# The forgetting attention's projections and attention given out ahead of the selecting attention's

## The chip, the cores and the metric

The kernel runs on one NeuronCore of a Trainium2 chip. The metric is the device time of one execution in microseconds. The kernel before took 1939.16 us, the median of three runs (1939.14 to 1940.99).

## The reference

The reference runs two layers of a first block and then a second block over one sequence of 256 tokens, 1024 wide, in fp32. The change lies in the first block. There a normed row x is multiplied with one wide matrix `w_in` (1024 x 3404), whose columns are cut into the inputs of four attentions of 4 heads x 64:

- A, the selecting attention: q, k, v (columns 0 to 767) and an indexer with 8 heads (768 to 1351). `score = sum_h iw_h * relu(iq_h . ik)`; of each row only the 64 best of its earlier keys take part in the softmax.
- B, the forgetting attention: q, k, v (1352 to 2119) and four columns b (2120 to 2123); the log of a sigmoid of b is summed along the sequence, and the difference of the sums at query and key is added to the logits.
- C, the differential attention (2124 to 2891): two softmaxes on 32 dimensions, the first minus lambda times the second, times v, then an rmsnorm per head.
- D, a sliding window of 128 keys with a sink (2892 to 3403).

The four outputs, side by side 1024 wide (`mix`: A, B, C, D), go through `w_out`, a norm and the residual; then come a 4096-wide MLP with squared relu, and a gated per-layer input.

## The kernel before, in words

The tokens are two row tiles (t = 0, 1) of 128. A weight is loaded in pieces of 1024 columns a partition (`wraw`, SP's queue, 4 buffers) and split in two fp32r parts: `whi` by ACT (L102) and the rest `wlo` by DVE (L103), 6 buffers each. The activations are held transposed and split in the same way (`phl`). A projection `proj(c0, n)` (L268) makes three matmuls per 128 rows of the weight (hi x hi, lo x hi, hi x lo): 24 for a row tile, 48 in all, into one of four accumulating PSUM banks per row tile. Another four banks serve everything else.

The side work, the attentions, are Python generators, put into a list by `push`. Each `mm_tok` advances the first two of the list by one step after 12 matmuls (`tick`), so attention steps are strewn in between the matmuls of the projection that follows; `until` steps them to their end. The list that results is put in order per engine by a scheduler, and each engine executes its instructions in that order: an instruction that waits holds all that stand behind it on its engine.

In `layer1` the order before is: the indexer's projections (768 and 1280), whose rope (L485 to L488) and transposes give `iqT` and `ikT` (L363); `index(t)` is pushed, which makes the index scores (matmul L517, relu L520, weighted sums L523), then takes the best 64 in eight rounds of MAX8 and MATCH_REPLACE8 on DVE (L529, L530), and turns the rest into a mask (L533, L534). Then come A's q, k (`proj(0, 512)`) and v, and A's attention is pushed; then the b columns and C's q (`proj(2120, 260)`), B's k, v (`proj(1608, 512)`), and B's attention is pushed; then C and D. An attention's step makes scores (L386), adds the mask and takes the maximum (L387, DVE), exponentials (L398, ACT), transposes of the probabilities (L411, copied by L413) and the product with v (L419). When A and B are done, `transpose_in` (L249; the split copies are L230 and L231) turns their part of `mix` for `w_out`; C's output goes through its norm (L574) first.

Of the kernel before, what the change touches and what calls it, by code (L numbers as in the profile page):

```python
# [17 lines left out]
P = 128  # L18
# [111 lines left out]
class Net:  # L130
# [448 lines left out]
    def layer1(self, i, xT):  # L579
# [20 lines left out]
        def proj(c0, n, get=None):  # L600
            get = get or self.w.cols(w_in, c0, n)
            res = []
            for t in range(NT):
                ps = self.bank(self.acc)[:, :n]
                n0 = 6 if self.early else KT
                self.mm_tok(ps, xT, t, range(n0), get, stop=n0 == KT)
                self.flush()
                if n0 < KT:
                    self.mm_tok(ps, xT, t, range(n0, KT), get, start=False)
                self.early = False  # L610
                res.append(ps)
            return res

        def keep(tag, ps, n, t):
            o = wk.tile([P, 256], F32, name=tag, tag=tag)[:, :n]
            nc.scalar.activation(o, ps, AF.Copy, scale=rstd[t])
            return o

        def roped(tag, pss, n, d):
            res = []  # L620
            for t in range(NT):
                o = wk.tile([P, 512 if n == 512 else 256], F32, name=tag, tag=tag)[:, :n]
                self.rope(o, pss[t], d, t)
                res.append(o)
            return res

        def q_alone(q, rows=64):

            qT = [wk.tile([P, 2, 2, P], F32, name="qT", tag="qT") for _ in range(64 // rows)]
            self.tr_alone(lambda r: qT[r // 2][:, r % 2], q, 2, rows)  # L630
            return qT

        def qT_kT(q, k):
            kT = wk.tile([P, 2, S], F32, name="kT", tag="kT")
            qT = []
            for t in range(NT):
                if q:
                    qT += q_alone(q[t])
                self.tr_heads(kT, k[t], t, 2)
            return qT, kT  # L640

        mix = [wk.tile([P, D], F32, name="mix", tag="mix") for _ in range(NT)]
        each = lambda f: [f(t) for t in range(NT)]


        ps = proj(768, 512, self.first if i == 0 else None)
# [4 lines left out]
        ps = proj(1280, 328, self.second if i == 0 else None)  # L651
# [11 lines left out]
        sel = [None] * NT  # L663
# [2 lines left out]
        if i == 0:  # L666
            self.setup1b()
        self.pin(nc.scalar.preload_act_table_set("natural_log_exp_and_others"))
        ps = proj(0, 512)
        q = roped("rq", [p[:, :256] for p in ps], 256, 64)  # L670
        k = roped("rk", [p[:, 256:] for p in ps], 256, 64)
        qTa, kTa = qT_kT(q, k)
        ps = proj(512, 256)
        va = each(lambda t: keep("v", ps[t], 256, t))

        def att_a(t):
            yield from self.attend(t, qTa, kTa, va, lambda h: h, lambda h: sel[t][:, :(t + 1) * P], mix[t][:, 0:256])

        gen_a = self.chain(*each(att_a))
        self.push(gen_a)  # L680


        ps = proj(2120, 260)
        nlf = []
# [13 lines left out]
        ps = proj(1608, 512)  # L698
# [4 lines left out]
        def att_b():  # L703
            pc = self.bank()
            nc.tensor.matmul(pc[:, 0:4], self.upper[:, :P], nlf[0], start=True, stop=True)
            nc.tensor.matmul(pc[:, 4:8], self.upper[:, P:], nlf[0], start=True, stop=False)
            nc.tensor.matmul(pc[:, 4:8], self.upper[:, :P], nlf[1], start=False, stop=True)
            ncum = self.small.tile([P, 2, 4], F32, name="ncum", tag="ncum")
            nc.vector.tensor_copy(ncum, pc[:, :8].rearrange("p (t h) -> p t h", t=2))
            dec = [wk.tile([P, 4, (t + 1) * P], F32, name="dec", tag=f"df{t}") for t in range(NT)]  # L710
            for h in range(4):
                if h % 2 == 0:
                    pr = self.bank()
                o = pr[:, (h % 2) * S:(h % 2 + 1) * S]
                nc.tensor.matmul(o, nlf[0][:, h:h + 1].to_broadcast([P, P]), self.upper, start=True, stop=False,
                                 skip_group_check=True)
                nc.tensor.matmul(o[:, P:], nlf[1][:, h:h + 1].to_broadcast([P, P]), self.upper[:, :P], start=False,
                                 stop=True, skip_group_check=True)
                for t in range(NT):
                    nk = (t + 1) * P  # L720
                    nc.vector.scalar_tensor_tensor(dec[t][:, h, :], o[:, :nk], ncum[:, t, h:h + 1],
                                                   self.causal[:, S - nk:], op0=ALU.subtract, op1=ALU.add)
                if h == 1:
                    yield
            yield
            for t in range(NT):
                yield from self.attend(t, qTb, kTb, vb, lambda h: h, lambda h: dec[t][:, h, :], mix[t][:, 256:512])
                yield
                if t == 0:
                    self.transpose_in(mix[t][:, :512], mT, t, 4)  # L730

        mT = self.new_parts(KT)
        gen_b = att_b()
        self.push(gen_b)


        ps = proj(2380, 512)
# [8 lines left out]
        ps = proj(2892, 512)  # L746
# [172 lines left out]
        for t in range(NT):  # L919
            ps = [self.bank() for _ in range(2)]  # L920
# [581 lines left out]
```

## Time and profile before

| | |
|---|---|
| median of 3 runs | 1939.16 us (1939.14 to 1940.99) |
| profiled execution, its own time | 1937.16 us |
| span in the trace | 1935.4 us |
| mean granted TensorE clock | 0.988 |
| PE busy / weight loads | 97% / 83% of the span |
| DVE / ACT / POOL busy | 68% / 54% / 4% |
| stretch of the attentions in layer 0 / 1 | about 31 to 176 us / 418 to 555 us of the span |

PE is TensorE's matmuls, PEld its weight loads, DVE VectorE, ACT ScalarE. Matmuls overlap: the duration of a row of PE includes its fill, so what a matmul costs in a row of them is the distance between starts. A row's bracket gives the idle time of the engine in front of it and what ended that.

### The profile page before, as it was taken

To read this page: it belongs to the slowest core of one execution; us is meant where nothing else is said; L and a number is where in the kernel's file an instruction comes from. 1 tells how busy PE (TensorE), PEld (TensorE's weight loads), DVE (VectorE), ACT (ScalarE), POOL (GpSimd) and SP (SyncE) were. 2 spreads that over 40 slices of the span, in tenths; PEclk is the share of its full clock that TensorE was granted. 3 is DMA by queue.
4 is the path that set the end of the run, shared out by engine and by line. 5 is a ranking of instruction groups with operands and counts; after the bars stand their busy time and mean duration, and the time that the engine had idled before them with its cause. 6 is when DMAs were issued, how large, how long until landed. Compare 5 with 4: busy or idle time off the path is not lost.

```text
span 1935.4 us, 27780 instructions
## 1 busy us (share of the span) xinstructions
PE 1877.3 (97%) x10282; PEld 1614.0 (83%) x10282; DVE 1306.8 (68%) x2456; ACT 1035.9 (54%) x1743; POOL 77.8 (4%) x127
## 2 busy tenths in 40 slices
PE   7898999999989999999999999999999999999997
PEld 6787878887878888888888988887988888988886
DVE  6866756687776666558666667566558666677555
ACT  5555544564654545566555655554565555655552
POOL 2000000000000000100000000000000000000000
PEclk9998999999999999999999999999999999999999
DMA  7433676554335555655555656664454555656662
GB/s 214 131 112 97 209 241 210 164 179 133 110 123 186 180 203 158 188 162 162 176 179 181 221 174 211 195 186 141 155 170 155 182 182 172 206 168 217 186 193 89
DMA packets 187132, 334.00 MB, mean 173 GB/s; under 512 B 11622, under 2 KB 109078, under 8 KB 186612
## 3 DMA queue, kind: packets, MB, share of 16 engines
q1 hardware_dynamic: 180160, 308.94, 50.4%
q0 software_dynamic: 6528, 23.18, 3.9%
q8 instruction: 81, 1.33, 0.3%
q14 instruction: 55, 0.45, 0.1%
q10 hardware_dynamic: 308, 0.10, 0.0%
HBM read 331.10 MB, written 4.62 MB: 173 GB/s over the span
## 4 chain that ended last, share of the span: by engine, by line
PE 83%; DVE 7%; DMA 4%; ACT 4%; issue 2%; POOL 0%; DVEq 0%; SPq 0%; ACTq 0%; POOLq 0%
PE bank L325 23%; PE bank L284 20%; PE bank L268 13%; PE bank L327 12%; DMA wraw<-in_w_in_dram 3%; DVE wlo L103 2%; PE bank L386 2%; PE bank L419 2%; PE bank L315 2%; PE bank L314 2%; PE bank L313 2%; ACT whi L102 1%; PE bank L249 1%; ACT pr L398 1%; PE bank L411 1%
## 5 line engine op out<-in xcount | busy, mean ns | idle before, releaser
L103 DVE TENSOR_TENSOR wlo<-wraw,whi 128x1024 fp32r<-128x1024 f32 (+1 forms) x628 | 711.0, 1147 | 328.7 <-ACT whi L102 238.6
L102 ACT ACTIVATE whi<-wraw 128x1024 fp32r<-128x1024 f32 (+1 forms) x628 | 608.9, 997 | 346.1 <-PE bank L284 110.2
L325 PE MATMUL bank<-phl,whi 128*128 128x512 f32 x2080 | 532.3, 395 | 0.4 <-ACT whi L102 0.4
L325 PEld LDWEIGHTS bank<-phl,whi 128*128 128x128 f32 x2080 | 374.9, 189 | 69.1 <-ACT whi L102 1.2
L284 PE MATMUL bank<-whi,phl 128*128 128x512 f32 x1280 | 358.2, 395 | 1.7 <-ACT phl L230 1.0
L268 PE MATMUL bank<-whi,phl 128*128 128x512 f32 (+4 forms) x1152 | 341.2, 378 | 4.3 <-ACT whi L102 2.2
L327 PEld LDWEIGHTS bank<-phl,wlo 128*128 128x128 f32 x2080 | 284.2, 190 | 23.2 <-DVE wlo L103 2.7
L327 PE MATMUL bank<-phl,wlo 128*128 128x256 f32 x2080 | 291.8, 283 | 0.6 <-DVE wlo L103 0.6
L284 PEld LDWEIGHTS bank<-whi,phl 128*128 128x128 f32 x1280 | 237.4, 189 | 53.3 <-ACT phl L230 2.9
L268 PEld LDWEIGHTS bank<-whi,phl 128*128 128x128 f32 x1152 | 210.9, 191 | 34.9 <-ACT phl L230 3.8
L268 PE MATMUL bank<-wlo,phl 128*128 128x512 f32 (+4 forms) x576 | 215.4, 376 | 2.4 <-DVE wlo L103 2.3
L284 PE MATMUL bank<-wlo,phl 128*128 128x512 f32 x640 | 206.2, 394 | 0.1
L284 PEld LDWEIGHTS bank<-wlo,phl 128*128 128x128 f32 x640 | 120.2, 188 | 28.8 <-DVE wlo L103 2.8
L268 PEld LDWEIGHTS bank<-wlo,phl 128*128 128x128 f32 x576 | 110.0, 191 | 18.2 <-DVE wlo L103 4.3
L315 PE MATMUL bank<-phl,wlo 128*128 128x256 f32 x304 | 86.3, 284 | 0.0
L314 PE MATMUL bank<-phl,whi 128*128 128x256 f32 x304 | 86.1, 283 | 0.0
L225 POOL TENSOR_TENSOR ry<-ry,mhalf 128x1 f32<-128x1 f32 (+1 forms) x40 | 32.9, 824 | 1309.1 <-DVE ry L224 1301.6
L313 PE MATMUL bank<-phl,whi 128*128 128x256 f32 x304 | 85.5, 281 | 0.0
L313 PEld LDWEIGHTS bank<-phl,whi 128*128 128x128 f32 x304 | 57.7, 190 | 0.2
L314 PEld LDWEIGHTS bank<-phl,whi 128*128 128x128 f32 x304 | 57.3, 189 | 0.2
L315 PEld LDWEIGHTS bank<-phl,wlo 128*128 128x128 f32 x304 | 57.5, 189 | 0.0
L230 ACT ACTIVATE phl<-bank 128x512 fp32r<-128x512 f32 (+2 forms) x60 | 32.8, 571 | 44.0 <-PE bank L249 43.6
(301 smaller groups left out, 1720.9 us busy)
## 6 DMA issues: line engine op xcount, KB each, us to landing
wraw<-in_w_in_dram SPq DMA_DIRECT2D x172, 512.0 KB, 4.6
wraw<-in_w_mlp_up_dram SPq DMA_DIRECT2D x64, 512.0 KB, 4.6
wraw<-in_w_mlp_down_dram SPq DMA_DIRECT2D x64, 512.0 KB, 4.5
wraw<-in_w_ffn_gate_dram SPq DMA_DIRECT2D x44, 512.0 KB, 4.7
wraw<-in_w_ffn_up_dram SPq DMA_DIRECT2D x44, 512.0 KB, 4.5
wraw<-in_w_ffn_down_dram SPq DMA_DIRECT2D x44, 512.0 KB, 4.4
wraw<-in_w_in_dram SPq DMA_DIRECT2D x54, 384.0 KB, 3.8
wraw<-in_w_out_dram SPq DMA_DIRECT2D x32, 512.0 KB, 4.3
```

The costliest lines, as they stand in the source:

```text
L102: first = nc.scalar.activation(hi[:, :n], src, AF.Copy)
L103: ins = nc.vector.tensor_tensor(lo[:, :n], src, hi[:, :n].bitcast(F32), op=ALU.subtract)
L225: nc.gpsimd.tensor_tensor(y, y, self.mhalf[:, :n], op=ALU.pow)
L268: self.order(nc.tensor.matmul(ps, self.part(parts, kt)[x][:, sl], get(kt + kbase)[w], start=start and n == 0, stop=stop and n == len(terms ...
L284: ins = nc.tensor.matmul(pss[j], self.part(parts, kt)[x][:, sl], get(kt + kbase)[w][:, j * 512:(j + 1) * 512], start=start and n == 0, sto ...
L313: self.order(nc.tensor.matmul(ps, wh, xh, start=first, stop=False, **kw), n == 0)
L314: nc.tensor.matmul(ps, wh, xl, start=False, stop=False, **kw)
L315: nc.tensor.matmul(ps, wl, xh, start=False, stop=last, **kw)
L325: self.order(nc.tensor.matmul(flat, get(kt)[0][:, c:c + P], both, start=n == 0, stop=False), n == 0)
L327: nc.tensor.matmul(ps[:, 0], get(kt)[1][:, c:c + P], self.part(parts, kt)[0], start=False, stop=n == len(kts) - 1)
L386: nc.tensor.matmul(o, qs(h), ks(h), start=True, stop=True)
L419: nc.tensor.matmul(po[:, h * 64:(h + 1) * 64], pts[kb][:, h, :], v(kb, h), start=kb == 0, stop=kb == t)
```

## The change

The lines that make A's projections and push its attention move behind those of B. The transposes of `mix[0]`'s first half, which B's attention made for A's and B's columns together, are cut in two: B's generator turns columns 256 to 511, A's turns 0 to 255.

```diff
--- before.py
+++ after.py
@@ -666,19 +666,6 @@
         if i == 0:
             self.setup1b()
         self.pin(nc.scalar.preload_act_table_set("natural_log_exp_and_others"))
-        ps = proj(0, 512)
-        q = roped("rq", [p[:, :256] for p in ps], 256, 64)
-        k = roped("rk", [p[:, 256:] for p in ps], 256, 64)
-        qTa, kTa = qT_kT(q, k)
-        ps = proj(512, 256)
-        va = each(lambda t: keep("v", ps[t], 256, t))
-
-        def att_a(t):
-            yield from self.attend(t, qTa, kTa, va, lambda h: h, lambda h: sel[t][:, :(t + 1) * P], mix[t][:, 0:256])
-
-        gen_a = self.chain(*each(att_a))
-        self.push(gen_a)
-
 
         ps = proj(2120, 260)
         nlf = []
@@ -727,11 +714,28 @@
                 yield from self.attend(t, qTb, kTb, vb, lambda h: h, lambda h: dec[t][:, h, :], mix[t][:, 256:512])
                 yield
                 if t == 0:
-                    self.transpose_in(mix[t][:, :512], mT, t, 4)
+                    self.transpose_in(mix[t][:, 256:512], mT, t, 2, 2)
 
         mT = self.new_parts(KT)
         gen_b = att_b()
         self.push(gen_b)
+
+
+        ps = proj(0, 512)
+        q = roped("rq", [p[:, :256] for p in ps], 256, 64)
+        k = roped("rk", [p[:, 256:] for p in ps], 256, 64)
+        qTa, kTa = qT_kT(q, k)
+        ps = proj(512, 256)
+        va = each(lambda t: keep("v", ps[t], 256, t))
+
+        def att_a(t):
+            yield from self.attend(t, qTa, kTa, va, lambda h: h, lambda h: sel[t][:, :(t + 1) * P], mix[t][:, 0:256])
+            if t == 0:
+                yield
+                self.transpose_in(mix[t][:, :256], mT, t, 2)
+
+        gen_a = self.chain(*each(att_a))
+        self.push(gen_a)
 
 
         ps = proj(2380, 512)
```

PE in layer 0, where the selection's mask is first met, before: bank_758 and bank_806 are the two row tiles of `proj(2120, 260)` (wlo_749 and wlo_755 are its last splits), kT_613, pr_790 and v_730 to A's attention, bank_919 and bank_970 to `proj(1608, 512)`.

```order
L268 MATMUL bank_919<-whi_897,phl_114 128x512
L268 MATMUL bank_970<-whi_897,phl_114 128x512
L268 MATMUL bank_758<-wlo_749,phl_115 128x260
L268 MATMUL bank_758<-whi_754,phl_115 128x260 x2
L268 MATMUL bank_806<-wlo_749,phl_115 128x260
L268 MATMUL bank_806<-whi_754,phl_115 128x260 x2
L268 MATMUL bank_758<-wlo_755,phl_115 128x260
L268 MATMUL bank_806<-wlo_755,phl_115 128x260
L386 MATMUL bank_791<-kT_613,qT_614 128x128
L386 MATMUL bank_796<-kT_613,qT_614 128x128
L411 MATMUL bank_819<-ident_79,pr_790 128x128 x4
L419 MATMUL bank_838<-v_730,pt_824 128x64 x4
```

After, where PE first needs a split that DVE makes behind the rounds: bank_737 to bank_747 are transposes for B's q and k, nlf and bank_866 B's sums and first scores, bank_782 and bank_828 the two row tiles of `proj(0, 512)` with its first split wlo_761.

```order
L268 MATMUL bank_782<-whi_760,phl_114 128x512
L268 MATMUL bank_828<-whi_760,phl_114 128x512
L362 MATMUL bank_752<-ident_79,bk_729 128x128 x2
L692 MATMUL bank_811<-nlf_591,c_upper_288 128x4
L693 MATMUL bank_811<-nlf_591,c_upper_288 128x4
L694 MATMUL bank_811<-nlf_600,c_upper_288 128x4
L702 MATMUL bank_819<-c_upper_288,nlf_591 128x256
L704 MATMUL bank_819<-c_upper_288,nlf_600 128x128
L702 MATMUL bank_841<-c_upper_288,nlf_591 128x256
L704 MATMUL bank_841<-c_upper_288,nlf_600 128x128
L386 MATMUL bank_866<-kT_735,qT_736 128x128
L268 MATMUL bank_782<-wlo_761,phl_114 128x512
```

Before, A's scores, transposes and product stand directly in PE's way at the mask; now what stands there are B's sums and first score, and then A's own projection.

DVE in layer 0, the end of the eight rounds (score_494 and score_502 are the two row tiles), before, with the splits of `proj(2120, 260)` between them and A's first scores behind.

```order
L530 MATCH_REPLACE score_494<-top_659,score_494 128x128
L529 MAX top_664<-score_502 128x8
L103 TENSOR_TENSOR wlo_749<-wraw_746,whi_748 128x260
L530 MATCH_REPLACE score_502<-top_664,score_502 128x256
L103 TENSOR_TENSOR wlo_755<-wraw_752,whi_754 128x260
L533 TENSOR_SCALAR score_494<-score_494 128x128
L533 TENSOR_SCALAR score_502<-score_502 128x256
L534 TENSOR_TENSOR score_494<-score_494,c_causal_287 128x128
L534 TENSOR_TENSOR score_502<-score_502,c_causal_287 128x256
L387 ISA pr_790,mx_789<-bank_791,score_494 128x128
```

After, the same place, with the splits of `proj(0, 512)` (wlo_761 to wlo_779) behind the rounds.

```order
L530 MATCH_REPLACE score_502<-top_661,score_502 128x256
L529 MAX top_656<-score_494 128x8
L529 MAX top_661<-score_502 128x8
L530 MATCH_REPLACE score_494<-top_656,score_494 128x128
L530 MATCH_REPLACE score_502<-top_661,score_502 128x256
L103 TENSOR_TENSOR wlo_761<-wraw_758,whi_760 128x1024
L103 TENSOR_TENSOR wlo_767<-wraw_764,whi_766 128x1024
L103 TENSOR_TENSOR wlo_773<-wraw_770,whi_772 128x1024
L103 TENSOR_TENSOR wlo_779<-wraw_776,whi_778 128x1024
L533 TENSOR_SCALAR score_494<-score_494 128x128
L533 TENSOR_SCALAR score_502<-score_502 128x256
L534 TENSOR_TENSOR score_494<-score_494,c_causal_287 128x128
```

Two 260-wide splits that stood at the last round are now ahead of the rounds, and four 1024-wide ones stand between the last round and the masks.

PE at the end of layer 0's attentions (second row tile), before: bank_1727 is D's product, bank_1745 C's.

```order
L419 MATMUL bank_1727<-v_1399,pt_1705 128x64
L419 MATMUL bank_1727<-v_1397,pt_1698 128x64
L419 MATMUL bank_1727<-v_1399,pt_1705 128x64
L419 MATMUL bank_1745<-v_1164,pt_1718 128x64
L419 MATMUL bank_1745<-v_1166,pt_1725 128x64
L419 MATMUL bank_1745<-v_1164,pt_1718 128x64
L419 MATMUL bank_1745<-v_1166,pt_1725 128x64
L419 MATMUL bank_1745<-v_1164,pt_1718 128x64
L419 MATMUL bank_1745<-v_1166,pt_1725 128x64
L419 MATMUL bank_1745<-v_1164,pt_1718 128x64
L419 MATMUL bank_1745<-v_1166,pt_1725 128x64
L249 MATMUL bank_1781<-ident_79,mix_166 128x128 x4
```

After: pr_1663 are D's probabilities, bank_1730 is C's product, bank_1750 D's.

```order
L411 MATMUL bank_1710<-ident_79,pr_1663 128x128
L411 MATMUL bank_1717<-ident_79,pr_1663 128x128
L419 MATMUL bank_1730<-v_1203,pt_1708 128x64
L419 MATMUL bank_1750<-v_1429,pt_1715 128x64
L419 MATMUL bank_1750<-v_1431,pt_1722 128x64
L419 MATMUL bank_1750<-v_1429,pt_1715 128x64
L419 MATMUL bank_1750<-v_1431,pt_1722 128x64
L419 MATMUL bank_1750<-v_1429,pt_1715 128x64
L419 MATMUL bank_1750<-v_1431,pt_1722 128x64
L419 MATMUL bank_1750<-v_1429,pt_1715 128x64
L419 MATMUL bank_1750<-v_1431,pt_1722 128x64
L249 MATMUL bank_1784<-ident_79,mix_166 128x128 x4
```

C's product, which stood last ahead of the transposes of mix, now stands among D's transposes and ahead of D's product.

## Rows read from the trace of the kernel before

**Rows 1.** PE, DVE, ACT in stretches of layer 0: busy us (count), PEld between; PEclk; DMA

```profile
50.00:70.00 20.00, 17.82 (x131) 16.51 (x129) 19.79 (x81) 7.77 (x16) 0.00 (x0) 1.00 0.23 63
70.00:80.00 10.00, 7.10 (x24) 5.51 (x25) 7.21 (x33) 5.57 (x16) 0.00 (x0) 0.74 0.44 151
80.00:100.00 20.00, 20.00 (x105) 16.68 (x105) 12.00 (x19) 11.89 (x25) 0.00 (x0) 0.96 0.71 228
...
160.00:175.00 15.00, 9.07 (x53) 8.20 (x54) 6.77 (x23) 6.17 (x21) 1.55 (x2) 0.73 0.00 1
```

**Rows 2.** timeline of PE, layer 0 selection: start, us, instruction, [idle before]

```profile
65.73 0.85 PE L268 MATMUL bank<-whi,phl 128*128 128x260 f32 x4
68.39 0.39 PE L268 MATMUL bank<-wlo,phl 128*128 128x260 f32 x1 [1.81 <-DVE wlo L103]
...
72.25 1.48 PE L411 MATMUL bank<-ident,pr 128*128 128x128 f32 x4 [1.32 <-ACT pr L398]
...
81.49 1.12 PE L268 MATMUL bank<-whi,phl 128*128 128x512 f32 x4
```

**Rows 3.** timeline of PE, distances that give prices

```profile
82.68 0.62 PE L268 MATMUL bank<-whi,phl 128*128 128x512 f32 x2
...
83.37 0.62 PE L268 MATMUL bank<-whi,phl 128*128 128x512 f32 x2
...
61.23 0.64 PE L268 MATMUL bank<-whi,phl 128*128 128x260 f32 x4
61.70 0.28 PE L268 MATMUL bank<-wlo,phl 128*128 128x260 f32 x1
...
48.69 1.47 PE L517 MATMUL bank<-ikT,iqT 128*128 128x128 f32 x8
...
49.80 0.82 PE L268 MATMUL bank<-whi,phl 128*128 128x512 f32 x2
```

**Rows 4.** timeline of PE, layer 1 selection

```profile
448.70 0.62 PE L268 MATMUL bank<-whi,phl 128*128 128x512 f32 x2
...
461.06 1.26 PE L268 MATMUL bank<-whi,phl 128*128 128x512 f32 x4
```

**Rows 5.** timeline of PE, end of the attentions, layer 0, then layer 1

```profile
164.00 2.26 PE L419 MATMUL bank<-v,pt 128*128 128x64 f32 x16 [0.48 <-ACT pt L413]
...
166.78 3.73 PE L419 MATMUL bank<-v,pt 128*128 128x64 f32 x16 [0.52 <-ACT pt L413]
...
173.93 1.12 PE L249 MATMUL bank<-ident,mix 128*128 128x128 f32 x4 [3.42 <-DVE mix L574]
...
552.94 1.11 PE L249 MATMUL bank<-ident,mix 128*128 128x128 f32 x4 [3.42 <-DVE mix L574]
```

**Rows 6.** timeline of PE, first matmuls of A's projection, both layers

```profile
31.17 0.47 PE L268 MATMUL bank<-whi,phl 128*128 128x512 f32 x1
...
417.89 0.39 PE L268 MATMUL bank<-whi,phl 128*128 128x512 f32 x1
```

**Rows 7.** DVE's timeline, rope and selection; last, grouped lines: splits, mean ns

```profile
57.13 0.28 DVE L486 TENSOR_TENSOR rope<-bank,cr 128x128 f32<-128x128 f32 x1
...
58.19 0.28 DVE L486 TENSOR_TENSOR rope<-bank,cr 128x128 f32<-128x128 f32 x1
...
58.59 0.28 DVE L529 MAX8 top<-score 128x8 f32<-128x128 f32 x1
...
59.38 0.61 DVE L529 MAX8 top<-score 128x8 f32<-128x256 f32 x2
...
60.55 0.61 DVE L529 MAX8 top<-score 128x8 f32<-128x256 f32 x2
...
440.16 0.28 DVE L529 MAX8 top<-score 128x8 f32<-128x128 f32 x1
...
L103 DVE TENSOR_TENSOR wlo<-wraw,whi 128x1024 fp32r<-128x1024 f32 x516 | 622.6, 1220 | 287.3 <-ACT whi L102 210.4 <-PE bank L327 70.0 <-issue 1.3
```

**Rows 8.** timeline of PE, layer 0, first index scores

```profile
39.41 1.23 PE L517 MATMUL bank<-ikT,iqT 128*128 128x128 f32 x6 [3.27 <-ACT ikT L363]
```

## Prediction

> **What bounds the kernel now.** I read first the page's busy shares, then windows over the attention stretch of both layers, PE's waits, the timelines of PE and DVE at the places these named, and last the grouped lines for prices. PE is busy 97% of the span (the table above), so only the places where it is not can give time back without removing work. The windows find two such places in layer 0 [rows 1], and layer 1 has their like. At 50 to 80 us of the span DVE is busy 19.79 of 20 us while PE has gaps, and then PE's granted clock is 0.74 of 2.4 GHz, that is partly the 1.2 GHz level; at 80 to 100 it is full again. At 160 to 175 PE is busy 9.07 of 15 us, with nothing coming by DMA.
>
> The first place is the selection: eight rounds of MAX8 and MATCH_REPLACE8 for both row tiles, then the attention that needs them. In PE's timeline of layer 0 [rows 2] the last cheap work starts at 65.73; then PE waits on a split that DVE holds behind the rounds (1.81), then on the masked scores and what follows from them (1.32 on their exponentials), and the full-width projection work is back at 81.49. Those 15.76 us hold 12 matmuls 260 wide, 12 x 0.118 = 1.4; four passes of scores, four transposes and eight of the value product at 128 or less, 16 x 0.11 = 1.8; eight 256-wide score passes at twice that, 1.8; three 512-wide matmuls, 0.7. That is 5.7, so 10.1 us are lost. (0.23 for a 512-wide matmul, 0.118 for a 260-wide one: three and four of them between starts [rows 3]; 0.11 for 128 wide is my rounding of the 260-wide one down.) Layer 1 [rows 4]: 448.70 to 461.06 is 12.36 us, with 4.7 of work by the same count; 7.7 lost.
>
> The second place is the end of the attention [rows 5]: the sliding-window product (164.00), the differential product (166.78), and then the transposes of mix wait 3.42 us on DVE, on the norm of the differential output; layer 1 shows the same 3.42 [rows 5].
>
> **The change part by part.** In PE's order A's two projections (0 and 512) and its attention stand behind B's two (2120 and 1608). No matmul is added, and none removed.
>
> *Selection.* What PE can do between the last indexer projection and the first matmul that needs something behind the rounds is now: 48 matmuls 260 wide, 48 x 0.118 = 5.7; four index groups at 1.11 [rows 3] 4.4; 48 matmuls 512 wide, 11.0; eight transposes, the cumulative sums and the first score, about 12 short passes at no more than 0.118, 1.4; two 512-wide ones, 0.5. Together 23.0 us. That work starts where the first matmul of A's projection starts now: at 31.17 and 417.89 [rows 6].
> - When the rounds start: of DVE's work ahead of them, four splits for A's q and k, two for A's v (all 1024 wide) and two 780 wide are replaced by two 780, two 260 and four 1024 wide; A's four rope groups (1.06 each, from one L486 to that of the next group) become two, and eight instructions of four columns come in (about 0.13 each, an estimate: under half of the 0.28 of the 128-wide one). Splits: 6 x 1.22 + 2 x 0.96 = 9.2 before, 4 x 1.22 + 2 x 0.96 + 2 x 0.40 = 7.6 after (the shorter ones scaled by width) [rows 7]; rope 4.2 before, 2.1 after; 1.0 in. DVE has 2.7 less to do, and before it was at MAX8 at 58.59 with hardly a gap: 55.9 in layer 0. In layer 1 DVE waits for the index groups, and these come 48 x (0.23 - 0.118) = 5.4 earlier: between 440.16 - 5.4 = 434.8 and 440.16 - 2.7 = 437.5 [rows 7].
> - When they end: a round takes 1.17 (59.38 to 60.55), eight 9.4; the first of A's splits stands right behind, 1.2 more [rows 7]. So 66.5 in layer 0, 445.4 to 448.1 in layer 1.
> - When PE gets there: layer 0, 31.17 + 23.0 + 2.0 for the transposes of the indexer's q and k, + 3.3 for the wait on ikT that stands in front of the first index group [rows 8] and some 2.2 of half clock behind it (an estimate: six passes there take 1.23, twice their price, and I let that last some 4.4 us) = 61.7. Layer 1, 417.89 + 23.0 + 1.1 = 442.0.
> - What is left to wait: 4.8 in layer 0, 3.4 to 6.1 in layer 1 (I take 4.8), and 1 us each of half clock behind it; 5.8 lost, against 10.1 and 7.7. Gain 4.3 and 1.9. A's scores, which PE now meets only after two 512-wide passes and A's v, no longer wait on the masks: that is inside the two differences. Bounds: 0 when the wait only moves, 10.1 and 7.7 when all of it is covered.
>
> On the page "Perfetto Trace Analysis" of the Trainium skill, section "Identifying the Most-Contended Engine", the engine of highest occupancy is to be improved first, and TensorE is to be judged by its weight loads. By the window 50 to 70, DVE (19.79) stands over PE's weight loads (16.51), so the rule speaks for no gain there, 0 in place of 6.2 us; the same page's "Optimization Strategy" allows that interleaving stretches with different bounds helps, and the trace shows such stretches side by side: DVE full at 50 to 70, PE full at 80 to 100 [rows 1].
>
> *Waits that the order adds.* The four splits of A's projection (4 x 1.22) stand in DVE's queue between the rounds and the masks, and behind them B's decay and scores. PE uses a split in 6 x 0.23 = 1.4 us, more than the 1.22 that DVE needs for one, so once the first is there they don't hold PE; B's first decay rows come some 7 us after the rounds, under 24 matmuls 512 wide (5.5) and A's second pass. I take 0; 2 us a layer at worst.
>
> *DMA.* The weight loads follow the new order on SP's queue: 260-wide columns first, which is less data ahead of the wait on ikT. I take no change, with bounds of -3.3 (the wait gone) and +3.3 (doubled).
>
> *The split transposes.* Two groups of 256 columns in place of one of 512: one instruction more on ACT and on DVE a layer, each under the 1.22 of a 1024-wide split, beside w_out and projection work: 0, at worst 1.2 a layer.
>
> *End of the attention.* In the new PE order the differential transposes come before the last w_out matmuls, the differential product is interleaved with the sliding-window transposes, and the sliding-window product is last. Behind the differential product then stand 2.26 us of work plus its 0.48 of wait [rows 5], under which the norm can run: the 3.42 falls to about 1.0, the sliding-window attention's own short chain (a reciprocal and a product on DVE). Gain 2.4 a layer, 4.8 in all. Bounds: all of 3.42 and the 0.52, 3.9 a layer; or -1, if the earlier differential transposes wait for DVE, which is then behind on the differential's subtraction.
>
> **Sum.** 4.3 + 1.9 + 4.8 = 11.0. The profiled execution took 1937.16, its span of 1935.4 and 1.8 around it; 1937.2 - 11.0 = 1926.2. It stands 2.0 under the median of the runs, 1939.16, so the forecast on that footing is 1928.2, rounded 1928.
>
> **The rivals.**
> 1. *DVE sets the stretch, and the wait moves.* No DVE instruction goes; if its whole chain from the first index scores to the last mask is what ends each time, PE's loss is the same later. For: 19.79 of 20. Against: after the rounds DVE is busy 7.21 of 10 [rows 1], so it has room right behind. Selection 0 and the end 0 to 3: 1936 to 1939, within 0.2%.
> 2. *Slower: the rounds catch PE with nothing in hand.* PE comes to A's first split just as MAX8 starts, because the wait at ikT or for B's second split has already delayed the index groups and with them the rounds. Then PE waits 9.4 + 1.2 and about 3 more at half clock, 13.6 a layer, in place of 10.1 and 7.7: +9.4, less about 2.4 at the end; 1946. It decides when PE is less than about 2 us behind MAX8. For: in layer 0 B's second split stands among the last index sums on DVE, some 6 us before the rounds (three splits, two rope groups). Against: 23 us of work in hand against the 9.4.
> 3. *All is covered.* The rounds end before PE arrives in both layers, and the end keeps its 3.4 a layer: 17.8 + 6.8 = 24.6; 1915. Against: it needs MAX8 5 us earlier than DVE's count gives.
>
> **How the numbers follow.** Two runs of this kernel can be told apart at about 0.2%, 3.9 us. Forecast 0.60, rival 1 0.16, rival 2 0.10, rival 3 0.14. Faster by over 0.2% is the forecast and rival 3, 0.74; same 0.16; slower 0.10. The range goes from rival 3's 1915 to 1941, past rival 1 and the unknown waits; rival 2 is left out, with a little of the low end. The forecast's own range is 1920 to 1934.
>
> **What would show it.** Right: PE's wait on wlo (L103) in front of the first 512-wide matmuls of A, 3 to 6 us a layer; none to speak of on A's masked scores; the granted clock of the stretch above 0.9; the wait of L249 on mix near 1 us, on L494 rather than L574. Wrong: a wait over 9 us on wlo; a wait on mix still at 3.4; new waits on differential transposes (L411 on df) or on B's decay (L386); the index groups or the wait on ikT coming later than now.

## The result, and the profile after

The changed kernel takes 1914.68 us (median of 4 runs, 1913.21 to 1915.68), the kernel before 1939.15 in the same comparison: a ratio of 0.9883, 95% interval 0.9867 to 0.9898. It is 24.5 us faster, where 11.0 were forecast, with 1915 as the low end of the range. A second comparison, further down, gave 1917.07 for it, 21.4 less than the kernel before: sizes of a few us are to be read with that in mind. The profiled execution's span went from 1935.4 to 1911.4.

Where the 24.0 us of the span come from is read at three marks that both kernels have: TensorE's first matmul after the indexer's projections, the first matmul of `w_out` (L284), and the first transposes of `xg` (L249), just behind those of mix. The rows of PE's timeline, before (the first mark is in [rows 6]):

```profile
130.36 0.71 PE L284 MATMUL bank<-whi,phl 128*128 128x512 f32 x2
...
174.84 1.49 PE L249 MATMUL bank<-ident,xg 128*128 128x128 f32 x6
...
510.73 0.70 PE L284 MATMUL bank<-whi,phl 128*128 128x512 f32 x2
...
553.85 1.49 PE L249 MATMUL bank<-ident,xg 128*128 128x128 f32 x6
```

and after:

```profile
30.95 0.29 PE L268 MATMUL bank<-whi,phl 128*128 128x260 f32 x1
...
122.88 0.82 PE L284 MATMUL bank<-whi,phl 128*128 128x512 f32 x2
...
162.31 1.48 PE L249 MATMUL bank<-ident,xg 128*128 128x128 f32 x6
...
405.54 0.28 PE L268 MATMUL bank<-whi,phl 128*128 128x260 f32 x1
...
491.40 0.81 PE L284 MATMUL bank<-whi,phl 128*128 128x512 f32 x2
...
530.82 1.49 PE L249 MATMUL bank<-ident,xg 128*128 128x128 f32 x6
```

Call the first stretch of a layer the front (all projections, and the selection) and the second the end. The differences of these starts:

| us | front, layer 0 | end, layer 0 | front, layer 1 | end, layer 1 |
|---|---|---|---|---|
| before | 99.2 | 44.5 | 92.8 | 43.1 |
| after | 91.9 | 39.4 | 85.9 | 39.4 |
| gain | 7.3 | 5.1 | 7.0 | 3.7 |

That is 23.0; the last 1.0 lies behind the second end.

A fourth mark stands further on, where the half clock that follows the last wait is over: the first transposes of `rlu` in the MLP (L249). Before, layer 0 and layer 1:

```profile
194.66 0.60 PE L249 MATMUL bank<-ident,rlu 128*128 128x128 f32 x4
...
573.59 0.60 PE L249 MATMUL bank<-ident,rlu 128*128 128x128 f32 x4
```

and after:

```profile
183.08 0.60 PE L249 MATMUL bank<-ident,rlu 128*128 128x128 f32 x4
...
551.73 0.60 PE L249 MATMUL bank<-ident,rlu 128*128 128x128 f32 x4
```

From `w_out` to it take 64.3 and 62.9 before and 60.2 and 60.3 after. By this mark the ends gain 4.1 and 2.5, so 1.0 and 1.2 of the 5.1 and 3.7 go back behind the transposes of `xg`; part of that is scatter, for a second profile of the changed kernel has 59.1 and 59.6.

**The front after.** Windows of layer 0, columns as in [rows 1]:

```profile
50.00:70.00 20.00, 17.56 (x86) 14.24 (x85) 19.28 (x67) 7.86 (x15) 0.00 (x0) 1.00 0.50 148
70.00:80.00 10.00, 9.91 (x61) 8.55 (x60) 9.45 (x32) 5.68 (x10) 0.00 (x0) 1.00 0.61 197
```

DVE is as full as before (19.28 of 20, before 19.79), but 70 to 80 is now full on PE too, and the granted clock stays at 1.00, where it was 0.74 [rows 1]. DVE's timeline, the first MAX8 of layer 0 and A's four splits; then, in layer 1, two of B's splits, the first MAX8 and A's first split:

```profile
53.65 0.62 DVE L529 MAX8 top<-score 128x8 f32<-128x128 f32 x2
...
63.05 4.62 DVE L103 TENSOR_TENSOR wlo<-wraw,whi 128x1024 fp32r<-128x1024 f32 x4
...
406.91 2.56 DVE L103 TENSOR_TENSOR wlo<-wraw,whi 128x1024 fp32r<-128x1024 f32 x2 [0.21 <-ACT whi L102]
...
421.33 0.28 DVE L529 MAX8 top<-score 128x8 f32<-128x128 f32 x1
...
430.67 1.21 DVE L103 TENSOR_TENSOR wlo<-wraw,whi 128x1024 fp32r<-128x1024 f32 x1
```

and PE where it needs the first of these splits, with the first index scores of layer 0 in front:

```profile
37.15 0.71 PE L517 MATMUL bank<-ikT,iqT 128*128 128x128 f32 x4 [1.58 <-ACT ikT L363]
...
63.07 0.39 PE L386 MATMUL bank<-kT,qT 128*128 128x128 f32 x2
64.32 0.50 PE L268 MATMUL bank<-wlo,phl 128*128 128x512 f32 x1 [0.86 <-DVE wlo L103]
...
431.94 0.50 PE L268 MATMUL bank<-wlo,phl 128*128 128x512 f32 x1
```

In layer 0 PE waits 0.86 us for the split, in layer 1 it comes just when the split is done and waits for nothing. The waits of [rows 2] on A's masked scores and exponentials are gone, and the 3.27 of [rows 8] is 1.58.

**The end after.** PE's waits in the end of layer 0 (the line that waited, what for, us in total, times, longest):

```profile
PE bank L249 <- DVE mix L574: 3.1, 1, 3.1
PE bank L419 <- ACT pt L413: 0.6, 2, 0.4
PE bank L411 <- ACT pr L398: 0.6, 1, 0.6
PE bank L386 <- DVE mx L387: 0.4, 1, 0.4
PE bank L284 <- ACT phl L230: 0.3, 1, 0.3
```

The same view before, 130 to 175 us:

```profile
PE bank L249 <- DVE mix L574: 3.4, 1, 3.4
PE bank L419 <- ACT pt L413: 1.7, 3, 0.7
PE bank L411 <- ACT pr L398: 1.6, 1, 1.6
PE bank L284 <- ACT phl L230: 0.3, 1, 0.3
```

The wait on mix, which I let fall to 1.0, is hardly shorter; those on exponentials (L398) and copies (L413) fell from 3.3 to 1.2. And the last product, which took 3.73 us for 16 passes at a lower clock in layer 0 [rows 5], takes 2.26; in layer 1 it took 2.37 before.

### The profile page after: what moved, and what is told of

Read it like the earlier page. It is cut to its first block, busy times and chain, and to the rows that moved or that the text cites. A ratio compares the mean times of both kernels' runs of the same rounds, so it can differ in the third digit from the quotient of the medians.

```text
span 1911.4 us, 27784 instructions
## 1 busy us (share of the span) xinstructions
PE 1865.5 (98%) x10282; PEld 1605.7 (84%) x10282; DVE 1304.1 (68%) x2458; ACT 1035.3 (54%) x1745; POOL 78.7 (4%) x127
## 4 chain that ended last, share of the span: by engine, by line
PE 85%; DVE 6%; DMA 4%; ACT 2%; issue 2%; POOL 0%; SPq 0%; DVEq 0%; ACTq 0%; POOLq 0%
PE bank L325 24%; PE bank L284 21%; PE bank L268 14%; PE bank L327 12%; DVE wlo L103 2%; PE bank L386 2%; DMA wraw<-in_w_in_dram 2%; PE bank L315 2%; PE bank L314 2%; PE bank L313 2%; PE bank L419 2%; PE bank L249 1%; PE bank L411 1%; PE bank L1259 1%; ACT whi L102 1%
## 5 line engine op out<-in xcount | busy, mean ns | idle before, releaser
L103 DVE TENSOR_TENSOR wlo<-wraw,whi 128x1024 fp32r<-128x1024 f32 (+2 forms) x628 | 711.2, 1148 | 322.7 <-ACT whi L102 231.3
L102 ACT ACTIVATE whi<-wraw 128x1024 fp32r<-128x1024 f32 (+2 forms) x628 | 608.7, 997 | 346.6 <-PE bank L284 112.7
L284 PE MATMUL bank<-whi,phl 128*128 128x512 f32 x1280 | 358.0, 395 | 1.0 <-ACT phl L230 1.0
L284 PEld LDWEIGHTS bank<-whi,phl 128*128 128x128 f32 x1280 | 237.7, 189 | 52.7 <-ACT phl L230 2.9
L284 PE MATMUL bank<-wlo,phl 128*128 128x512 f32 x640 | 206.3, 394 | 0.1
L284 PEld LDWEIGHTS bank<-wlo,phl 128*128 128x128 f32 x640 | 120.2, 188 | 28.7 <-DVE wlo L103 2.7
L225 POOL TENSOR_TENSOR ry<-ry,mhalf 128x1 f32<-128x1 f32 (+1 forms) x40 | 33.8, 846 | 1285.1 <-DVE ry L224 1277.6
L314 PE MATMUL bank<-phl,whi 128*128 128x256 f32 x304 | 86.1, 283 | 0.0
L313 PEld LDWEIGHTS bank<-phl,whi 128*128 128x128 f32 x304 | 57.7, 190 | 0.2
```

The lines of the kernel that those rows point to most:

```text
L102: first = nc.scalar.activation(hi[:, :n], src, AF.Copy)
L103: ins = nc.vector.tensor_tensor(lo[:, :n], src, hi[:, :n].bitcast(F32), op=ALU.subtract)
L225: nc.gpsimd.tensor_tensor(y, y, self.mhalf[:, :n], op=ALU.pow)
L284: ins = nc.tensor.matmul(pss[j], self.part(parts, kt)[x][:, sl], get(kt + kbase)[w][:, j * 512:(j + 1) * 512], start=start and n == 0, sto ...
L313: self.order(nc.tensor.matmul(ps, wh, xh, start=first, stop=False, **kw), n == 0)
L314: nc.tensor.matmul(ps, wh, xl, start=False, stop=False, **kw)
```

## The experiments

Fronts and ends below are measured at the same marks, in one profiled execution each; the fronts of the changed kernel and of the variants that leave its front alone lie between 91.5 and 94.5 in layer 0, with the first transfers, and between 85.9 and 86.5 in layer 1.

**One layer alone.** With a flag set to `i == 0`:

```diff
+        if b_first:
+            gen_b, cq = part_b()
+            gen_a = part_a()
+        else:
+            gen_a = part_a()
+            gen_b, cq = part_b()
```

> The new order in layer 0, the old one in layer 1. Theory S (each layer's selection wait is covered, and what was in front of it and behind it in that layer goes with it; between the first matmul that differs and the transposes of mix layer 0 is 12.3 us shorter, layer 1 10.7): 1939.2 - 12.3 = 1927, give or take 1.5. Rival L (most comes from layer 0's start, where the smaller loads come earlier and the clock does not fall): under 1922. If the layers were not additive, say because layer 0's end sets where layer 1's loads stand: over 1930.

1925.82 us, ratio 0.9937 (0.9922 to 0.9952). Layer 0 has the front and end of after (92.2 and 39.4), layer 1 those of before (93.5 and 43.0). The layers add up.

**C held back.** In the changed kernel the generators of C are pushed one by one:

```diff
-        for gen in gen_c:
-            self.push(gen)
+        self.push(gen_c[0])
...
         self.until(gen_a, gen_b)
+        self.push(gen_c[1])
```

> The changed kernel, but C's second row tile is not in the list until A and B are done, so that the end of the attention has its old order on TensorE (differential transposes among the sliding-window ones, differential product last). Theory S: the selection keeps its gain, the end loses 2 to 4 us a layer: 1919 to 1923, and the wait of L249 on mix is again 3.4. Rival E (the gain is mainly the end, C running ahead): 1928 or more.

1922.95 us, ratio 0.9916 (0.9900 to 0.9933). Fronts 91.0 and 85.2, as after and a little less; ends 44.8 and 45.3, 0.3 and 2.2 longer than before. So the order of the projections is worth 15.5 us by itself, and the end is a matter of C. As the code reads, B begins earlier and so leaves its place in the list earlier, C's second tile moves up, and its q and first scores are done before `w_out`. The selection has the larger part, not the end.

**Two rounds, before and after.**

```diff
+            if r < 2:
-            nc.vector.max(mx, score[:, :nk])
-            nc.vector.match_replace(score[:, :nk], mx, score[:, :nk], GONE)
+                nc.vector.max(mx, score[:, :nk])
+                nc.vector.match_replace(score[:, :nk], mx, score[:, :nk], GONE)
```

Before: 

> The kernel before with two of the eight rounds of the selection (it keeps 16 keys in place of 64), so 6 x 1.17 = 7.0 us less on VectorE ahead of the masks in each layer. Theory S: TensorE was waiting for the rounds, so the time falls by 5 to 7 us a layer, 1925 to 1929. Rival E: by less than 3 in all, 1936 or more.

After: 

> The changed kernel with two of the eight rounds. Theory S: the rounds are covered, only the 0.9 us wait for the first split of A's projection in layer 0 and what VectorE holds up right behind can go: 0 to 3 us less, 1912 to 1915. If the rounds still set the stretch (VectorE bound, the wait only moved): 5 us a layer less, 1905 or below.

Before with two rounds: 1921.72, ratio 0.9913 (0.9898 to 0.9928), 16.8 us less; fronts 90.5 and 84.9. After with two rounds: 1914.28, ratio 0.9873 (0.9859 to 0.9888), no difference from eight; fronts 89.8 and 86.1. This is the clearest pair: taking six rounds of 1.17 us a layer away gives the old order what the new order has with all eight, and gives the new one nothing. The gain in the old order, 8.4 a layer, is more than the 7.0 of the rounds, because the clock stays up too; windows of that run:

```profile
50.00:70.00 20.00, 19.97 (x147) 18.80 (x146) 19.20 (x66) 12.05 (x28) 0.00 (x0) 1.00 0.44 139
70.00:80.00 10.00, 10.00 (x54) 8.38 (x54) 8.28 (x25) 6.31 (x20) 0.00 (x0) 1.00 0.64 173
```

**Twelve rounds after** (`range(12)`, with as many steps of the generator).

> The changed kernel with twelve rounds of the selection in place of eight (it keeps 96 keys), 4 x 1.17 = 4.7 us more on VectorE a layer. If the cover ends just at eight, as the arrivals read (TensorE reached A's first split in layer 1 at the moment when it was done, in layer 0 0.9 us early): 4 to 5 us a layer more, 1922 to 1925. If there is room under the matmuls behind the rounds too: under 1919.

1929.41 us, ratio 0.9947 (0.9929 to 0.9965), 14.7 more than after; fronts 101.7 and 92.8, ends as after. I had expected the cover to end at eight, and it does, but the price is higher than the 4.7 us a layer of four rounds. In layer 1 the wait, and the window around it:

```profile
PE bank L268 <- DVE wlo L103: 3.7, 1, 3.7
```

```profile
440.00:460.00 20.00, 16.30 (x66) 13.31 (x67) 16.86 (x50) 5.68 (x7) 0.00 (x0) 0.83 0.41 131
```

Behind the wait 13 passes of 512 stand between 445.32 and 451.02, 5.7 us, which is 2.7 more than at 0.23 each: 3.7 of wait and 2.7 of clock make 6.4 of the 6.9 by which that front grew. In layer 0 the front grew by 9.8: its waits are 5.0 longer in all (on the splits 3.1, a new one on pt, L413, 1.7), and the clock falls there twice, to 0.83 over 60 to 80 and over 90 to 100. These waits were paid nearly twice.

**C two steps further in the kernel before.**

```diff
         self.until(gen_a, gen_b)
+        for _ in range(2):
+            next(gen_c[1])
```

> The kernel before, with C's second row tile advanced two steps (its q and its first scores) once A and B are done, as it comes out in the changed kernel; projections and selection as before. Theory S (the end gains from C being further along when w_out begins, apart from the selection): 3 to 4 us a layer, 1931 to 1933, and the wait of L411 on the exponentials (1.6) falls to about 0.6 in both layers. Rival: the end gains only because the whole stretch is less late on VectorE; then 1936 to 1939.

1927.65 us, ratio 0.9939 (0.9924 to 0.9954), 12.1 less where 6 to 8 were expected. Fronts 99.4 and 92.9, as before; ends 39.5 and 39.6. In the end of layer 0:

```profile
PE bank L386 <- DVE mx L387: 1.2, 2, 0.7
PE bank L284 <- ACT phl L230: 1.1, 2, 0.7
PE bank L419 <- ACT pt L413: 0.5, 1, 0.5
PE bank L249 <- DVE mix L494: 0.3, 1, 0.3
```

Here C's norm is hidden: what L249 waits for is D's product (L494), 0.3 us. C is further along than in the changed kernel, so the 15.5 and the 12.1 don't add to the 24.5. That the end gains by itself, with the selection untouched, is shown. The ends of 39.5 and 39.6 hold only 8.5 of it; from `w_out` to the fourth mark it is 58.1 and 58.2, 10.9 less than before, since behind the wait of 0.3 the clock stays at 1.00 (165 to 176 us), where before it is 0.50 at 174 to 176, behind the wait of 3.42.

**C one step further in the changed kernel** (`next(gen_c[1])` once, at the same place), and the same with the first tile's norm ahead of mix (below).

> The changed kernel with C's second row tile advanced one more step when A and B are done, so that its product comes ahead of the last w_out matmuls and its norm runs beside them. Expected: the wait of L249 on mix (3.1) turns into one on D's product of under 1 us, 2 to 3 us a layer less: 1909 to 1911. Rival: C's earlier VectorE work delays the masks and exponentials in front: 1913 to 1916.

> As the one with C one step further, and the first row tile's norm and its transposes (xg) ahead of those of mix. With the wait on mix gone there is little left for them to fill: 0 to 1 us below the one without, 1908 to 1911. If both gains add: 1906.

1915.48, ratio 0.9881 (0.9866 to 0.9896), no gain, and 1919.39, ratio 0.9904 (0.9882 to 0.9925). With the step the wait on mix is on L494, 2.2 and 1.3; the fronts grew by 1.1 and 1.8 and the ends came to 40.2 and 38.1. From `w_out` to the fourth mark it is 58.7 and 57.7, 1.5 and 2.7 less than in the changed kernel (0.4 and 1.9 less than in its second profile), and the fronts take 1.1 and 1.8 of that back. In the joint one, whose profile is of its slowest run (1925.05), L249 waits 2.3 and 2.4 for xg on DVE (L807), and 2.2 and 0.8 on L494 beside it. What helped the old order is worth nothing here.

**The wait on ikT,** after and before: ScalarE's splits of the next projection's weights go behind the copies of ikT in layer 0.

```diff
+        getb = self.w.cols(w_in, 1608, 512)
+        if i == 0:
+            self.behind(ikc, *self.w.his[-4:])
-        ps = proj(1608, 512)
+        ps = proj(1608, 512, getb)
```

After: 

> The changed kernel, with the split of B's k, v weights on ScalarE in layer 0 put behind the copies of ikT, so that these don't stand behind a transfer. Theory S (VectorE's chain to the rounds and to A's first split sets when layer 0 goes on): the 1.6 us wait on ikT goes, and half or more of it comes back as waits on wlo further on: 0 to 1 us less, 1913.5 to 1914.7. Rival T (the wait on ikT was paid in full): 1.6 us less or a little more, 1912.5 to 1913.

Before, with A's weights: 

> The kernel before, with the splits of A's q, k weights on ScalarE in layer 0 put behind the copies of ikT: the wait of 3.3 us on ikT and the half clock behind it, some 5.5 in all, should go. Theory S (in layer 0 VectorE's chain up to the masks sets when TensorE gets on, so the time comes back at the masks): 0 to 2 us less, 1937 to 1939. Rival T (it was paid in full): 4 us less or more, 1935 or below.

After: 1915.37, ratio 0.9878 (0.9863 to 0.9892): the wait is gone, 1.1 of waiting on whi has come. Before: 1937.27, ratio 1.000 (0.9991 to 1.001): the wait fell from 3.3 to 0.7, that on the masked maxima (L386 on mx) rose from 0.6 to 1.5, and the time is the same. Its first mark can't be compared, since two index groups moved ahead of A's projection. TensorE's waits from 28 to 82 us add up to 6.2, before to 8.2, but layer 0's 328-wide projection begins 1.1 later in this profile, and `w_out` at 130.22 where it was 130.36. In neither order does taking this wait away by itself shorten the time beyond the intervals, some 2 to 3 us.

**What the wait on mix costs.** C's scale ahead of D's product (norm first), and with the first tile's norm and its transposes ahead of those of mix (xg first):

```diff
+        if self.cn is not None:
+            self.behind(self.cn, z)
...
+        norm(0)
         self.transpose_in(mix[1][:, 512:], mT, 1, 4, 4)
         self.mm_pair(pss[1], mT, 1, range(4, 6), get, start=False, stop=False)
-        norm(0)
```

Here `cn` is the tensor_scalar of C's rsqrt (L224) and `z` D's last product (L494).

> The changed kernel, with the scale of C's norm (L224) ahead of D's last product (L494) on VectorE for the second row tile. If the wait of L249 on mix (3.1) is C's norm standing behind D's product, it falls by 1.0 to 1.1 a layer to about 2.1: 1912.5. If D's product or the gpsimd power (1.45 us) sets it anyway: no change, 1914 to 1915.

> As the kernel with the norm first, and the first row tile's post-attention norm with its transposes (xg, L249) given out ahead of the transposes of mix, which puts 16 passes of 0.11 into the wait. Expected: a further 1 to 2 us a layer less, 1909 to 1911. Rival: the norm's own VectorE work (two of 0.69, two of 0.75) delays C's norm by what the transposes fill: 1912 to 1914.

1916.07 (ratio 0.9878, 0.9864 to 0.9893) and 1909.31 (0.9853, 0.9831 to 0.9875). As the first of these left open whether the wait counts at all, four kernels were measured side by side:

Changed kernel: 

> The changed kernel itself, as the reference of the next three: 1913 to 1916.

Norm first: 

> C's scale (L224) ahead of D's product (L494) on VectorE, once more. Theory N (the wait on mix is paid for as it stands): 2 x 0.9 = 1.8 us below the changed kernel. Theory X (what counts is TensorE's idle time together with the half clock that follows it): under 1 us.

Both: 

> Both, once more: 4 to 6 us below the changed kernel by either theory.

xg first alone: 

> Only xg first: its 16 passes fill 1.8 us of the 3.1 us wait. Theory N: 2 x 1.8 = 3.5 us below the changed kernel, and about 1.8 above the joint one. Theory X: as low as the joint one, within 1 us.

| | median us | ratio to before (95%) |
|---|---|---|
| changed kernel | 1917.07 | 0.9894 (0.9879 to 0.9909) |
| norm first | 1915.12 | 0.9889 (0.9874 to 0.9903) |
| xg first | 1910.85 | 0.9865 (0.9850 to 0.9880) |
| both | 1909.29 | 0.9854 (0.9837 to 0.9870) |

Both together are faster than the changed kernel beyond its interval, by 7.8 us here; this is the best version found. xg first is 6.2 below it by the medians, where filling 1.8 us of a wait in two layers makes 3.5, but the intervals touch, and the traces put only a part of the 6.2 where the edit is. From `w_out` to the fourth mark:

| us | layer 0 | layer 1 |
|---|---|---|
| changed kernel, first profile | 60.2 | 60.3 |
| changed kernel, this one | 59.1 | 59.6 |
| norm first | 59.1 | 59.4 |
| xg first | 57.4 | 59.5 |
| both | 56.5 | 58.1 |
| both, the earlier profile | 58.0 | 56.6 |

In the two layers together xg first saves 1.8 there, or 3.6 against the first profile, and both edits 4.1 to 6.0. Most of the rest of the 6.2 lies behind the second layer, from the fourth mark of layer 1 to the end of the span: 1364.9 in this profile of the changed kernel, 1360.4 with xg first, but 1359.7 in the first profile of the changed kernel, with no edit in that stretch. So the 3.5 of Theory N is not refuted, and the 6.2 is in part scatter.

What the clock has in it is not settled. Windows around the wait in layer 0, 160 to 170, of the changed kernel and then of xg first:

```profile
160.00:170.00 10.00, 7.74 (x34) 6.73 (x35) 6.24 (x9) 3.94 (x6) 3.04 (x4) 0.83 0.28 85
```

```profile
160.00:170.00 10.00, 7.79 (x38) 6.36 (x39) 6.62 (x10) 4.31 (x7) 3.14 (x4) 1.00 0.34 96
```

and around the same place in layer 1, again the changed kernel and then xg first:

```profile
528.00:538.00 10.00, 8.06 (x34) 6.99 (x35) 5.81 (x8) 3.92 (x5) 2.20 (x3) 0.71 0.27 79
```

```profile
525.00:535.00 10.00, 7.84 (x29) 6.10 (x28) 4.92 (x9) 2.85 (x4) 2.78 (x3) 0.66 0.26 78
```

The clock stayed up in layer 0, where xg first gains 1.7, and fell in layer 1, where it gains nothing. With the transposes of xg ahead L249 waits 0.90 for xg and then 1.64 and 1.27 for mix, in place of 3.13. Norm first cut the wait to 2.3 and gained 2 us at most, inside the intervals.

## Why the prediction was wrong

The direction and both places were right; the sum was less than half of what came, and the time lies just under the range. Of the 12.0 that the sum lacks against the 23.0 of the marks, 8.1 are the fronts' and 4.0 the ends'.

- *"What is left to wait: 4.8 in layer 0, 3.4 to 6.1 in layer 1, and 1 us each of half clock."* This is the step that failed: measured are 0.86 and none, and no half clock. It is a difference of two arrivals, and both were off by about 2 us, each towards a shorter wait.
  - The rounds were early: MAX8 at 53.65, not 55.9; in layer 1 (everything is 12.35 earlier there) at 421.33, not 422.5 to 425.1. In layer 0 I had read DVE before as having "hardly a gap" ahead of MAX8. From 50 on that holds, but between 35 and 49 its idle times add up to 5.0 (2.95 of it at 43.88, on rl of ScalarE), and after they are 3.3, with the shorter wait on ikT, which I had held unchanged. In layer 1 the index groups came the 5.4 earlier that I had counted (the last L517 at 416.55, before at 434.31), and behind the last of them DVE took 4.8 to MAX8 where it had taken 5.9. I had let the two set the ends of a range and taken its middle; they add, to 6.5.
  - PE was late. From its start to A's first split it took 32.3 us in layer 0, of which 4.5 were waits, so 27.8 of work where I had 25.0; in layer 1 26.4 with 0.9 of waits, 25.5 for 24.1. B's transposes, cumulative sums and first score, put at 1.4, took 3.3 and 2.3, and some 0.2 us behind each index group were left out.
- *The front's gain* was to be 4.3 and 1.9; C held back shows 8.2 and 7.6 (99.2 to 91.0, 92.8 to 85.2), and two rounds in the old order 8.7 and 7.9. So of the loss that I had read, 10.1 and 7.7, layer 1 lost all, and layer 0 some 8. Which of the waits in its new front (1.58 on ikT, twice 0.86 on splits, 0.93 on bk, 0.66 on qT, 0.51 on w) keep the rest is not shown.
- *ikT:* held at no change; it fell to 1.58 with the clock at 1.00 behind it. The two runs on it show that this alone was not paid for.
- *"The 3.42 falls to about 1.0."* It fell to 3.13. The cover came, but I had taken the chain behind C's product as it was, and it grew. The rows of PE, ACT, DVE and GpSimd in after, layer 0, by their start:

```profile
155.29 0.33 PE L419 MATMUL bank<-v,pt 128*128 128x64 f32 x2
156.03 2.26 PE L419 MATMUL bank<-v,pt 128*128 128x64 f32 x16 [0.41 <-ACT pt L413]
156.35 0.39 ACT L568 ACTIVATE oc<-bank 128x256 f32<-128x256 f32 x1
157.24 0.41 DVE L571 TENSOR_REDUCE v<-ocs 128x4 f32<-128x256 f32 x1
158.34 0.42 DVE L494 TENSOR_TENSOR mix<-bank,rsum 128x256 f32<-128x256 f32 x1 [0.68 <-PE bank L419]
158.68 0.16 DVE L224 TENSOR_SCALAR ry<-v 128x4 f32<-128x4 f32 x1
158.74 0.75 DVE L806 SCALAR_TENSOR_TENSOR xg<-u,ry,xg 128x512 f32<-128x512 f32 x1
158.91 1.45 POOL L225 TENSOR_TENSOR ry<-ry,mhalf 128x4 f32<-128x4 f32 x1 [2.38 <-DVE ry L224]
160.40 0.43 DVE L573 TENSOR_TENSOR oc<-oc,ry 128x256 f32<-128x256 f32 x1 [0.91 <-POOL ry L225]
160.86 0.42 DVE L574 TENSOR_TENSOR mix<-oc,subln 128x256 f32<-128x256 f32 x1
```

C's product ends at 155.62 (the first row), mix is done at 161.28: 5.7 us, of which D's product (the second) covers 2.7; before the same chain takes 3.4 (170.51 to 173.87). Of the 2.3 more, 0.7 lie ahead of ACT's copy oc (L568), which stands behind the copies for D; 0.2 ahead of the reduction (L571); 1.0 between that and C's scale (L224), which stands on DVE behind D's product (L494) and so waits for PE; and 0.4 in the power on GpSimd, 1.45 for 1.02. Norm first took away 0.5 of the third and all of the fourth, 0.9 in all; the other terms are read from the rows and were not tested. The end gained 5.1 and 3.7 all the same, against 2.4 each: by waits on exponentials and copies that C's transposes and product now fill, in layer 0 by the product at full clock, and by C's q and first scores, which moved from the end to the front (0.9 and 0.6 us, the difference of the fronts with C held back). That the 2.5 of layer 1 at the fourth mark stands beside the 2.4 of the forecast is luck: the wait it was to come from is still there.
- *Rivals.* That DVE sets the stretch in the new order too is refuted: in after DVE is still at 19.28 of 20, the gain is there, and six rounds less on DVE give nothing more. The Trainium skill's "Perfetto Trace Analysis" (section "Identifying the Most-Contended Engine") would have one improve that engine first; these runs agree only for the old order, where less DVE work gave 16.8 us. Rival 2 was nowhere near. Rival 3, all covered, had the time (1915) and nearly the front, but its end was to lose all of its 3.4, which did not happen; that its sum meets the time is in part luck. At 0.14 it was given too little: two arrivals that I could not time to 2 us decided between it and the forecast, and the forecast took the worse half of both.

## What to carry to other kernels

Where a stall is the difference of two long counts, work it out with both counts off by a few us either way before fixing a likeliest value: here two errors of 2 us took a wait of 4.8 to 0.9 and to none. Price a wait of TensorE with the clock that falls behind it (here 6.4 us for 3.7), and set the mark that a stretch is measured to behind that half clock, or a shorter wait looks worth less than it is (8.5 in place of 10.9 with C two steps further). When work is moved behind a wait to cover it, look at what it puts into the other engines' queues ahead of the chain that is to be covered: here the cover came and the chain grew by 2.3. And in a list that advances two generators at a time, moving one also changes when the next ones start: a third of this gain came from C, which the edit does not name.

## What the runs showed of the hardware

- The granted clock fell around the longer waits of PE: to 0.83 over 20 us with a wait of 3.7; with the wait of 3.1 in layer 0, over 160 to 170, to 0.67 in one profile of the changed kernel and to 0.83 in another. With the wait broken into 0.9 and 1.6 by transposes it was 1.00 over the same 10 us, but with 0.9 and 1.3 in layer 1 it was 0.66, so the length of the wait alone did not decide it in these runs.
- The power of 128 x 4 on GpSimd (L225), the same instruction, took 1.45 us wherever VectorE had just begun the product xg (L806, 0.75, rows above) beside it, in both layers of the changed kernel, of its second profile and of xg first. Before, VectorE was idle beside it, and it took 1.02 and 1.01; with the norm first D's product (L494) stood beside it, and it took 1.01 to 1.02. No run changed this alone.
